# One decoder layer on one core: a planner's figure for GpSimd in the first phase, ranks of the steps around the filling products, and one product moved up in the feed-forward part

## The chip, the core and the metric

The kernel runs on one NeuronCore of a Trainium2 chip as one launch. The metric is the device time of the launch in microseconds (us), from the profiler's first to last instruction and what lies around it; lower is better. TensorE is called PE here, VectorE DVE, ScalarE ACT, GpSimd POOL, and SyncE, which issues most DMAs, SP.

## What is computed

One layer over 2048 positions of width 1024, in float32, batch 1. Cut to what matters:

```python
hn = rms_norm(x, norm1_g)
q, k, v, u = split(hn @ w_in)                    # 512 columns each
attn = diff_attention(rope(q), rope(k), v, lam)  # 4 heads, two causal softmax maps each, difference of the maps
attn = rms_norm(attn, subln_g) * 0.2
y = gelu(s5_scan(u))                             # 32 groups, 64 complex states each
ssm = y * sigmoid(y @ w_glu + b_glu)             # GLU
h = x + concat(attn, ssm) @ w_out                # output projection
hn = rms_norm(h, norm2_g)
h = h + (silu(hn @ w_gate) * (hn @ w_up)) @ w_down   # DFF = 2816
return rms_norm(h, final_g)
```

## The kernel before, in words

A float32 product is made of three single-pass products (`mm3`, lines 518 to 520): each operand is split into a high part, rounded to the fast type by ACT, and a low part, the difference, made by DVE or POOL. So every operand of PE costs an ACT step and a DVE or POOL step first.

**The planner.** Nothing is issued in the order in which it is written. Each step is a `Task` with its engine (or several to choose from), an estimated cost, the tasks that it depends on, the buffers that it takes and gives (`Ring`) and a rank `pri`. `Sched.run` simulates the engines while the program is built: for each engine it looks at the tasks that could start within 0.05 us of the earliest, takes the one of lowest `pri`, and emits it. The result is a fixed order for every engine; on the chip each engine works through its own list in order and waits where an operand isn't there. A task that may run on DVE or POOL goes where its estimated start plus weighted cost is lower (`choose`).

**First phase** (lines 550 to 1000; all its instructions are shown as line 364, which records them; `pri` -100 to -40). RMSNorm, transposes on PE, the projections of u, q, k and v, tables for the scan, and sixteen pairs of scan groups (`ssm_pair`). In a pair, PE makes a product z from operands that are loaded from DRAM (`uD`, `GD`), two multiplies by a table may go to DVE or POOL (`nc.any`), and six 128x256 multiplies and adds for the table are on POOL. `Rec.call` estimates each recorded instruction from its size.

**Second phase.** Attention has `pri` 0 to about 32: scores (lines 1199, 1200, 1203), the row maximum on DVE (1221), exp on ACT (1237), the difference of the two maps on DVE or POOL (1287 to 1291), transposes (1320), the low part on DVE (1329), the product with v, and the heads' norm (1364 to 1382). Its query tiles come by SP from `qD` into a ring of two buffers.

Beside it run the *filling products*, so called because their ranks, 1000 and more, let PE take them only where no attention product can start:
- `glu` (`pri` from 1000): load y, split it, 384 matmuls of 128x256, tanh, multiply (line 1523), store.
- `outproj` (`pri` from 2000): load w_out and split it (high part on ACT, low part on DVE, line 1589), load and split the mixed rows (1609, 1610), 768 matmuls of 128x512 into bank `fx` (after attention into the score banks too); twelve of them make a half tile, which DVE adds to the residual (1645). The first 384 are for the scan's half, the others for attention's half.
- `norm2`: for each of the 16 tiles after its attention half is added: store, square (1676), scale on DVE (1679), transpose on PE (1691), copy (1694), store to `nD`.

**Feed-forward** (`ffn`, `pri` from 10000). Two blocks of 1024 positions; each pair of weight tiles is multiplied by a block with seven products instead of eight (Strassen-Winograd): A11, S2, A12, S3, S1, A22, S4 by B11, T2, B21, T3, T1, B22, T4. A product is 12 matmuls of 128x512 in two tasks of six. Operands of the weights are made in `operands` (s1, s3, s2, s4 on DVE or POOL, lines 1899 to 1909; low parts in 1783 and 1787) and wait in the ring `Ar`; those of the block are made once per block (`inputs_first`, `inputs_second`; lines 1783 and 1796). `blocks` issues the products: A11 into a bank, ACT copies that bank (p1, line 1952), S2 goes to another bank and DVE adds p1 (u2, line 1946), and A12 is accumulated onto A11's bank, for which p1 must have been read. After the two blocks the same scheme runs over w_down in three chunks (`down`), with the final norm in the last.

Of the kernel before, what the change touches and what calls it, by code (L numbers as in the profile page):

```python
# [175 lines left out]
class Sched:  # L176
# [14 lines left out]
    def __call__(self, engs, cost, fn, *deps, take=(), give=(), pri=0.0, size=0, stream=0, of=(), bias=BIAS,  # L191
                 port=False):

        t = Task()
        t.port = port
        t.engs = {engs: cost} if isinstance(engs, str) else engs
        if engs == "pe":
            t.engs = {engs: cost * 1.02}
        else:
            t.engs = {e: c + STEP.get(e, 0.0) for e, c in t.engs.items()}  # L200
        t.fn, t.pri, t.take, t.give, t.size, t.bias = fn, pri, take, give, size, bias
        t.next, t.wait, t.ready, t.done, t.got = [], 0, 0.0, False, {}
        for r in take:
            r.queues.setdefault(stream, deque()).append(t)
        t.at, t.of = stream, [o for o in of if o is not None]
        for d in (*deps, *t.of):
            if d is None:
                continue
            if d.done:
                t.ready = max(t.ready, d.end)  # L210
            else:
                d.next.append(t)
                t.wait += 1
        self.left += 1
        if not t.wait:
            self.arm(t)
        return t
# [79 lines left out]
class Rec:  # L297
# [92 lines left out]
    def call(self, eng, f, args, kw):  # L390
        isap = self.isap
        outs = [kw[n] for n in ("out", "accum_out") if isap(kw.get(n))]
        rest = [x for n, x in kw.items() if n not in ("out", "accum_out") and isap(x)]
        pos = [x for x in args if isap(x)]
        if "out" not in kw:
            outs.append(pos.pop(0))
        ins = rest + pos
        free = lambda x: math.prod(n for _, n in list(x.ap)[1:])
        n = max([free(outs[0])] + ([free(i) for i in ins] if "reduce" in f else []))
        c = ("", f, outs, ins, args, kw)  # L400
        if eng == "pe":
            cost = n / 2400.0 + 0.0035
            if f == "transpose":
                cost = 0.108
            elif kw["rhs"].dtype == F32:
                cost = max(4 * cost, 0.215)
            if self.open and (sum(x[0] for x in self.open) + cost > 1.3
                              or kw.get("start") and self.where(self.open[-1][2][0]) != self.where(outs[0])
                              or self.open[-1][2][0].tensor.name != outs[0].tensor.name):
                self.flush()  # L410
            self.open.append((cost, f, outs, ins, args, kw))
            return None
        self.flush()
        if f == "dma_start":
            return self.task(("sp", 0.47), [c], size=math.prod(outs[0].shape) * 4)
        psum = [x.space == PSUM for x in (outs[0], *ins)]
        if f == "tensor_tensor_scan" or psum[0]:
            dve = 2.3e-3 * n + 0.03
        elif f in ("tensor_scalar", "memset"):
            dve = 0.75e-3 * n + 0.03  # L420
        else:
            dve = 1.06e-3 * n + 0.06 if any(psum) else 1.27e-3 * n + 0.02
        cost = dict(dve=dve, act=0.87e-3 * n + (0.26 if "accum_out" in kw else 0.08),
                    pool=(1.0e-3 if f == "tensor_scalar" else 0.3e-3 if f == "memset" else 2.0e-3) * n + 0.12)
        if kw.get("op") == ALU.pow:
            cost["pool"] += 0.25 + 0.09 * n
        port = f == "tensor_tensor" and not any(psum)
        if eng == "any":
            return self.task({e: cost[e] for e in ("dve", "pool")}, [c], bias=FAIR if self.fair else BIAS, port=port)
        return self.task((eng, cost[eng]), [c], port=port)  # L430
# [69 lines left out]
class K:  # L500
# [1254 lines left out]
    def ffn(self):  # L1755
# [9 lines left out]
        A11, S2, A12, S3, S1, A22, S4 = range(7)  # L1765
# [9 lines left out]
        def pri():  # L1775
            seq[0] += 0.01
            return seq[0]
# [143 lines left out]
        def blocks(ws, B, last, finish):  # L1921
# [22 lines left out]
            def add(x, y, *deps, to=None, give=True):  # L1944

                return S("dve", 1.042e-3 * w + 0.07, lambda t: v.tensor_tensor(  # L1946
                    out=(t if to is None else to).got[tm], in0=x.got[bank], in1=y.got[tm],
                    op=ALU.add), x, y, *deps, take=[tm] if to is None else [], give=[(bank, x)] if give else [], pri=pri())

            place = lambda own: lambda: own.got[tm]  # L1950
            x1 = product(A11)
            p1 = S("act", 0.88e-3 * w + 0.07, lambda t: a_.copy(out=t.got[tm], in_=x1.got[bank]), x1,
                   take=[tm], pri=pri())
            u2 = add(product(S2), p1)
            x2 = product(A12, x1, p1)
            S.join(*finish(0, 0, p1, lambda: x1.got[bank], x2, u2), give=[(bank, x1)])
            u3 = add(product(S3), u2)
            x5 = product(S1)
# [200 lines left out]
        for c, (lo, hi) in enumerate(CHUNKS):  # L2159
            ops = rows(c, 0)  # L2160
            W = columns(c, wide)
            if c == len(CHUNKS) - 1:
                fg.append(S("sp", 0.47, lambda t: nc.sync.dma_start(out=t.got[rawr], in_=A["final_g"]), take=[rawr],
                            pri=pri(), size=524288))
# [29 lines left out]
```

## Time and profile before

| | |
|---|---|
| median of 3 runs | 2428.8 us (2423.4 to 2435.64) |
| the profiled execution | 2427.17 us |
| its span, first to last instruction | 2425.1 us |
| PE busy | 2334.0 us |
| DVE, ACT, POOL busy | 1719.6, 1051.0, 725.1 us |
| mean granted clock of PE | 0.984 |

The profile is of one execution. A row of the waits says who waited for whom, how long in all, how often, and the longest. A row of the windows says, for a stretch, its length, PE's busy time with its matmuls, the granted clock (1.00 is full speed), the DMA engines' share and GB/s. A group's row gives line, engine, operation, out<-in, shapes and count, then busy us and mean ns, then the idle time of the engine before it and what ended it.

### The profile page before, as it was taken

What the parts mean: (1) busy time and instruction counts of PE and PEld (TensorE: products, weight loads), DVE (VectorE), ACT (ScalarE), POOL (GpSimd) and SP (SyncE); (2) the same over time, 40 slices, a digit from 0 to 9 for tenths busy, and PEclk for the clock granted to TensorE, in tenths of its full rate; (3) what the DMA queues carried; (4) which work ended last, traced back from release to release, by engine and by line L of the source; (5) the groups of instructions that cost most, each with busy time, mean ns of one, the idle gap of its engine ahead of it and who ended that gap; (6) DMA issues with size and microseconds to landing.
All of it is one profiled execution on the core that took longest, in us unless ns stands there. A gap on an engine that the chain in (4) does not pass through costs nothing.

```text
span 2425.1 us, 33919 instructions
## 1 busy us (share of the span) xinstructions
PE 2334.0 (96%) x11832; PEld 1958.8 (81%) x11832; DVE 1719.6 (71%) x2801; ACT 1051.0 (43%) x2103; POOL 725.1 (30%) x824
## 2 busy tenths in 40 slices
PE   7999999889999999998999999999999989999998
PEld 6887798878888888876888888788888868878886
DVE  7885775247887768648987666866666677686787
ACT  7222332247877776545332333533333242242343
POOL 4134675355666556545311000100000010010033
PEclk9999999999999999999999999999999999999999
DMA  6467675665566557786986222522322255574564
GB/s 216 133 189 219 220 223 165 202 215 165 191 197 193 194 188 243 228 293 228 304 270 224 86 83 87 204 92 72 95 85 79 87 179 168 172 258 162 201 213 158
DMA packets 312172, 435.33 MB, mean 180 GB/s; under 512 B 42240, under 2 KB 187712, under 8 KB 312000
## 3 DMA queue, kind: packets, MB, share of 16 engines
q1 hardware_dynamic: 309408, 428.71, 55.5%
q10 hardware_dynamic: 2592, 4.45, 0.5%
q8 instruction: 93, 1.52, 0.3%
q14 instruction: 79, 0.65, 0.1%
HBM read 287.66 MB, written 145.42 MB: 179 GB/s over the span
## 4 chain that ended last, share of the span: by engine, by line
PE 70%; DMA 6%; DVE 5%; issue 3%; ACT 2%; POOL 1%; SPq 0%; POOLq 0%; DVEq 0%; ACTq 0%
PE pair L518 9%; PE pair L519 9%; PE pair L520 9%; PE tp L519 4%; PE tp L520 4%; PE tp L518 4%; PE fx L518 4%; PE fx L519 4%; PE pair L364 4%; PE fx L520 4%; PE pv L518 3%; PE pv L519 3%; PE pv L520 3%; DMA hn<-qD 2%; PE tp L1320 2%
## 5 line engine op out<-in xcount | busy, mean ns | idle before, releaser
L1782 ACT CAST misc<-hn 128x512 fp32r<-128x512 f32 (+1 forms) x340 | 204.9, 609 | 482.8 <-PE pair L519 160.6
L519 PE MATMUL pair<-hn,misc 128*128 128x512 f32 x925 | 361.0, 390 | 6.5 <-DVE hn L1783 4.6
L518 PE MATMUL pair<-hn,misc 128*128 128x512 f32 x925 | 361.3, 391 | 3.2 <-DVE misc L1946 2.5
L520 PE MATMUL pair<-hn,misc 128*128 128x512 f32 x925 | 360.2, 389 | 0.0
L1783 DVE TENSOR_TENSOR misc<-hn,misc 128x512 fp32r<-128x512 f32 (+1 forms) x340 | 237.2, 702 | 82.8 <-ACT misc L1782 82.6
L364 PE MATMUL pair<-hn,misc 128*128 128x512 f32 x1152 | 281.7, 398 | 0.0
L1899 POOL TENSOR_TENSOR misc<-hn 128x512 f32<-128x512 f32 (+1 forms) x13 | 17.9, 1378 | 783.0 <-DVE misc L1783 638.2
L364 PEld LDWEIGHTS pair<-hn,misc 128*128 128x128 f32 x1152 | 214.5, 190 | 45.4 <-issue 2.4
L519 PEld LDWEIGHTS pair<-hn,misc 128*128 128x128 f32 x925 | 173.9, 188 | 44.4 <-DVE hn L1783 6.5
L518 PEld LDWEIGHTS pair<-hn,misc 128*128 128x128 f32 x925 | 174.0, 188 | 41.3 <-DVE misc L1946 3.3
L520 PEld LDWEIGHTS pair<-hn,misc 128*128 128x128 f32 x925 | 173.9, 188 | 36.0
L1221 DVE TENSOR_REDUCE small<-pair 128x1 f32<-128x1024 f32 (+7 forms) x160 | 158.2, 991 | 53.5 <-PE pair L1200 24.8
L1237 ACT ACTIVATE hn<-pair,small 128x1024 f32<-128x1024 f32 (+4 forms) x192 | 166.3, 868 | 59.9 <-DVE small L1228 29.1
L519 PE MATMUL tp<-hn,misc 128*128 128x512 f32 x454 | 178.1, 392 | 3.7 <-DVE hn L1783 3.7
L518 PE MATMUL tp<-hn,misc 128*128 128x512 f32 x454 | 177.8, 392 | 0.0
L520 PE MATMUL tp<-hn,misc 128*128 128x512 f32 x454 | 177.4, 391 | 0.0
L1946 DVE TENSOR_TENSOR misc<-pair,misc 128x512 f32<-128x512 f32 x110 | 75.9, 690 | 84.9 <-PE pair L520 84.6
L364 POOL TENSOR_TENSOR misc<-misc,misc 128x512 f32<-128x512 f32 (+1 forms) x71 | 83.9, 1183 | 166.9 <-DVE misc L364 134.1
L364 DVE TENSOR_TENSOR misc<-misc,misc 128x512 f32<-128x512 f32 (+7 forms) x111 | 92.6, 852 | 36.6 <-ACT misc L364 31.9
L1329 DVE TENSOR_TENSOR hn<-tp,hn 128x512 fp32r<-128x512 f32 x144 | 95.4, 684 | 29.0 <-ACT hn L1326 28.6
L364 POOL TENSOR_TENSOR misc<-misc 128x256 f32<-128x256 f32 (+1 forms) x128 | 100.1, 793 | 43.6 <-DVE misc L364 19.8
L364 PE MATMUL pair<-misc,hn 128*128 128x256 f32 x768 | 103.3, 292 | 8.8 <-DVE misc L364 8.8
(272 smaller groups left out, 5614.7 us busy)
## 6 DMA issues: line engine op xcount, KB each, us to landing
hn<-vD SPq DMA_DIRECT2D x48, 512.0 KB
hn<-kD SPq DMA_DIRECT2D x96, 256.0 KB
hn<-in_w_gate SPq DMA_DIRECT2D x44, 512.0 KB
hn<-in_w_up SPq DMA_DIRECT2D x44, 512.0 KB
fD<-misc SPq DMA_DIRECT2D x88, 256.0 KB
misc<-in_w_down SPq DMA_DIRECT2D x77, 256.0 KB
hn<-qD SPq DMA_DIRECT2D x128, 128.0 KB
hD<-misc SPq DMA_DIRECT2D x32, 512.0 KB
```

The source lines that it names most:

```text
L364: getattr(ENGINE[t.at](self.real), f)(*map(now, args), **{n: now(x) for n, x in kw.items()})
L518: nc.tensor.matmul(out, lhsT=ah, rhs=bh, start=start, stop=False, **k)
L519: nc.tensor.matmul(out, lhsT=ah, rhs=bl, start=False, stop=False, **k)
L520: nc.tensor.matmul(out, lhsT=al, rhs=bh, start=False, stop=stop, **k)
L1221: v.tensor_reduce(out=nl[:, i:i + 1], in_=x.got[sc][:, 0:w], axis=AX.X, op=ALU.max, negate=True)
L1237: a_.activation(out=z.got[rings[i]][:, 0:w], in_=x.got[sc][:, 512 * i:512 * i + w], func=AF.Exp, bias=st(n, n + 1), accum_out=acc)
L1320: nc.tensor.transpose(t4[:, kt, t], a[:, kc % 1024:kc % 1024 + 128], self.ident)
L1329: v.tensor_sub(out=y.got[zr][:, 1], in0=y.got[tp].rearrange("p (k q) -> p k q", k=2), in1=y.got[zr][:, 0].bitcast(F32))
L1782: hf = lambda t: a_.copy(out=dst(t)[0], in_=src())
L1783: lf = lambda t: (g_ if t.at == "pool" else v).tensor_sub(out=dst(t)[1], in0=src(), in1=dst(t)[0].bitcast(F32))
L1899: s1 = any_(n, lambda t, e: e.tensor_tensor(out=t.got[s1r][:, 0:n], in0=q(1, 0), in1=q(1, 1), op=ALU.add), *r, take=[s1r], pri=pri(), bias ...
L1946: return S("dve", 1.042e-3 * w + 0.07, lambda t: v.tensor_tensor(out=(t if to is None else to).got[tm], in0=x.got[bank], in1=y.got[tm], op ...
```

## The change

Three edits.
1. In `Sched.__call__`, every task with a rank from 1000 up to 3000 that isn't for PE gets the rank -1. So all DMAs, ACT, DVE and POOL steps of `glu`, `outproj` and `norm2` come ahead of attention's on their engines when both could start; their products on PE keep their ranks. The first phase's ranks (-100 to -40) stay ahead of both.
2. In `Rec.call`, the estimate of a recorded two-input instruction on POOL goes from 2.0 to 2.4 ns an element. Only the first phase is recorded.
3. In `blocks`, product A12 is written ahead of S2, so it has the lower rank. It still needs p1.

```diff
         t.fn, t.pri, t.take, t.give, t.size, t.bias = fn, pri, take, give, size, bias
+        if 1000 <= pri < 3000 and "pe" not in t.engs:
+            t.pri = -1.0
...
-                    pool=(1.0e-3 if f == "tensor_scalar" else 0.3e-3 if f == "memset" else 2.0e-3) * n + 0.12)
+                    pool=(1.0e-3 if f == "tensor_scalar" else 0.3e-3 if f == "memset" else 2.4e-3) * n + 0.12)
...
+            x2 = product(A12, x1, p1)
             u2 = add(product(S2), p1)
-            x2 = product(A12, x1, p1)
```

No instruction is added or removed; the planner gives every engine another order and some steps another engine. Lines after 201 are two higher in the changed kernel. Three places follow.

DVE in attention, where w_out's low parts (line 1589, `misc0`<-`misc2`) are made, between the last GLU step and the first add of a half tile. Before:

```order
L1589 SCALAR_TENSOR_TENSOR misc0_5783<-misc2_5785,misc0_5783 128x512
L1287 SCALAR_TENSOR_TENSOR hn31_4411<-hn31_4411,small_128 128x512
L1221 TENSOR_REDUCE small_128<-pair00_3730 128x1
L1589 SCALAR_TENSOR_TENSOR misc0_5783<-misc2_5785,misc0_5783 128x512
L1287 SCALAR_TENSOR_TENSOR hn31_4411<-hn31_4411,small_128 128x512
L1221 TENSOR_REDUCE small_128<-pair10_4451 128x1
L1329 TENSOR_TENSOR hn10_4054<-tp1_104,hn10_4054 128x512
L1329 TENSOR_TENSOR hn30_4410<-tp0_103,hn30_4410 128x512
L1228 TENSOR_TENSOR small_128<-small_128 128x1
L1589 SCALAR_TENSOR_TENSOR misc0_5783<-misc2_5785,misc0_5783 128x512
```

The changed kernel at the same step (line 1591):

```order
L1223 TENSOR_REDUCE small_128<-pair10_4465 128x1
L1230 TENSOR_TENSOR small_128<-small_128 128x1
L1591 SCALAR_TENSOR_TENSOR misc0_5564<-misc2_5566,misc0_5564 128x512 x4
L1591 SCALAR_TENSOR_TENSOR misc0_5564<-misc5_5569,misc0_5564 128x512 x2
L1591 SCALAR_TENSOR_TENSOR misc3_5567<-misc5_5569,misc3_5567 128x512
L1371 SCALAR_TENSOR_TENSOR small_128<-small_128 128x4
L1223 TENSOR_REDUCE small_128<-pair10_4465 128x1
L1373 SCALAR_TENSOR_TENSOR small_128<-small_128 128x4
L1230 TENSOR_TENSOR small_128<-small_128 128x1
```

The eight low parts stood among 27 rows, between attention's maxima (1221) and low parts (1329); now seven stand in a row, and the eighth a few rows on. From the last GLU multiply to the first add of a half tile it was 47 rows and is 31.

DVE at the start of the feed-forward part, where the block's operands are split (line 1783 into `hn00`, `hn10`: B11 and B21) beside the half tiles' adds (1645) and norm2's scaling (1679). Before:

```order
L1645 TENSOR_TENSOR misc2_5785<-pair10_9454,misc2_5785 128x512
L1783 TENSOR_TENSOR hn00_9652<-hn31_9659,hn00_9652 128x512
L1679 SCALAR_TENSOR_TENSOR misc1_5784<-misc2_5785,misc6_5789 128x1024
L1645 TENSOR_TENSOR misc5_5788<-pair11_9455,misc5_5788 128x512
L1783 TENSOR_TENSOR hn00_9652<-hn31_9659,hn00_9652 128x512
L1645 TENSOR_TENSOR misc5_5788<-pv_105,misc5_5788 128x512
L1783 TENSOR_TENSOR hn10_9654<-hn31_9659,hn10_9654 128x512
L1783 TENSOR_TENSOR hn00_9652<-hn31_9659,hn00_9652 128x512
```

The changed kernel (1647, 1681 and 1785 are the same three):

```order
L1647 TENSOR_TENSOR misc5_5569<-pv_105,misc5_5569 128x512
L1681 SCALAR_TENSOR_TENSOR misc1_5565<-misc2_5566,misc6_5570 128x1024
L1785 TENSOR_TENSOR hn10_9891<-hn31_9896,hn10_9891 128x512
L1647 TENSOR_TENSOR misc5_5569<-pair00_9664,misc5_5569 128x512
L1785 TENSOR_TENSOR hn00_9889<-hn31_9896,hn00_9889 128x512
L1785 TENSOR_TENSOR hn10_9891<-hn31_9896,hn10_9891 128x512
L1785 TENSOR_TENSOR hn00_9889<-hn31_9896,hn00_9889 128x512
L1785 TENSOR_TENSOR hn10_9891<-hn31_9896,hn10_9891 128x512
```

Between the first of these splits and the first add of the feed-forward part (1946) DVE had 53 steps for feed-forward operands, 18 adds and 10 scalings; now it has 48, 5 and 3. The other adds and scalings come earlier.

DVE in the middle of the first block, where the weights' sums are made (1899 is s1, 1901 is s3). Before:

```order
L1946 TENSOR_TENSOR misc6_10374<-pair10_9454,misc1_10373 128x512
L1783 TENSOR_TENSOR misc3_5786<-misc2_5785,misc3_5786 128x512
L1899 TENSOR_TENSOR misc2_5785<-hn31_9659 128x512
L1901 TENSOR_TENSOR hn31_9659<-hn31_9659 128x512
L1787 SCALAR_TENSOR_TENSOR misc3_5786<-hn31_9659,misc3_5786 128x512
L1946 TENSOR_TENSOR misc6_10374<-pair00_9448,misc6_10374 128x512
```

The changed kernel:

```order
L1785 TENSOR_TENSOR misc0_5564<-hn31_9896,misc0_5564 128x512
L1785 TENSOR_TENSOR misc0_5564<-misc2_5566,misc0_5564 128x512
L1948 TENSOR_TENSOR misc6_10351<-fx_106,misc1_10350 128x512
L1789 SCALAR_TENSOR_TENSOR misc0_5564<-hn31_9896,misc0_5564 128x512
L1903 TENSOR_TENSOR hn31_9896<-hn31_9896 128x512
L1948 TENSOR_TENSOR misc6_10351<-tp0_103,misc6_10351 128x512
```

s1 (now 1901) no longer stands ahead of s3 (now 1903): of the 60 sums s1 of 128x512, DVE had 53 and POOL 7; now DVE has 16 and POOL 44. On PE, the first half of S2, all of A12 and the second half of S2 now follow each other in many blocks.

## The prediction, made blind

> **What bounds the kernel now.** I read the page first, then PE's windows by stage, PE's waits, and the timeline at two gaps.
>
> ```profile
> PE 2334.0 (96%) x11832; PEld 1958.8 (81%) x11832; DVE 1719.6 (71%) x2801; ACT 1051.0 (43%) x2103; POOL 725.1 (30%) x824
> ```
>
> PE is busy for 96% of the span, and the change adds and removes no matmul. So only two things can be won or lost: PE's idle time, and matmuls at a lowered clock. The windows place both.
>
> ```profile
> core 0: us, PE busy (x), PEclk, DMA share, GB/s
> 180.00:300.00 120.00, 112.51 (x565) 0.96 0.72 219
> 300.00:430.00 130.00, 128.04 (x781) 0.99 0.64 193
> 430.00:500.00 70.00, 61.12 (x450) 0.95 0.70 213
> 500.00:640.00 140.00, 130.44 (x948) 0.98 0.55 170
> 640.00:668.00 28.00, 22.48 (x139) 0.88 0.82 264
> 668.00:975.00 307.00, 302.10 (x1869) 1.00 0.64 202
> 975.00:1010.00 35.00, 30.10 (x184) 0.90 0.84 251
> 1060.00:1160.00 100.00, 89.87 (x404) 0.95 0.77 256
> 1160.00:1550.00 390.00, 390.00 (x1721) 1.00 0.52 167
> 1550.00:1580.00 30.00, 28.05 (x116) 0.94 0.80 278
> 1580.00:1970.00 390.00, 390.00 (x1722) 1.00 0.29 88
> 1970.00:2010.00 40.00, 32.75 (x120) 0.91 0.65 214
> 2140.00:2180.00 40.00, 35.81 (x135) 0.87 0.69 232
> ```
>
> I call a stage's loss its idle time plus (1 - PEclk) times its length: what it would save if PE never stopped. First phase, 180 to 500: idle 7.5 + 2.0 + 8.9 and clock 4.8 + 1.3 + 3.5, 28 us. Attention's beginning, 500 to 668: idle 9.6 + 5.5, clock 2.8 + 3.4, 21 us. The rest of attention, 668 to 1010: 4.9 + 4.9 and 3.5, 13 us. The passage into the feed-forward part, 1060 to 1160: 10.1 and 5.0, 15 us. The feed-forward blocks have no loss in 780 of their 810 us; the joints at 1550, 1970 and 2140 lose 24 us together. A matmul of 128x512 takes 390 / 1721 = 0.227 us there, a product of twelve 2.72 us.
>
> The clock term needs its own look, at the joint at 1550: the timeline's row at the gap, then a window just behind it.
>
> ```profile
> 1562.64 0.79 PE L519 MATMUL fx<-hn,misc 128*128 128x512 f32 x1 [1.90 <-DVE hn L1783]
> 1562.50:1565.90 3.40, 3.26 (x8) 0.50 0.84 276
> ```
>
> One gap of 1.90 us is followed by 3.4 us at half clock: 1.7 us more are lost. [...] The sum goes by the rows.
>
> PE's waits name the causes: 500 to 640 first (two rows), then 640 to 668 (one), then 180 to 500 (three).
>
> ```profile
> PE pair L1199 <- DMA hn<-qD: 4.7, 5, 1.8
> PE pair L1199 <- ACT hn L1237: 3.3, 2, 2.8
> ...
> PE pair L1199 <- ACT hn L1237: 4.2, 2, 2.3
> ...
> PE pair L364 <- DVE misc L364: 8.8, 5, 3.0
> PE pv L364 <- DMA misc<-uD: 5.6, 8, 1.3
> PE pv L364 <- DMA misc<-GD: 3.5, 1, 3.5
> ```
>
> They are many small waits at places where PE's list stood on an operand that came later than planned. None is a stage's steady limit.
>
> **Part 1, ranks.** No work goes away; steps of the filling products overtake attention's on DVE, ACT, POOL and SP. What stands behind an overtaking step waits for its length, 0.7 us on DVE, and attention behind it; PE covers that as long as a filling product can start. The clearest place is 640 to 668. There GLU was done and the output projection hadn't begun, as DVE's rows of the three kinds show (last GLU multiply, first low part of w_out, first add of a half tile):
>
> ```profile
> L1523 DVE SCALAR_TENSOR_TENSOR misc<-misc x6: 678/702/1111, 516.1 to 637.2; 128x512 f32<-128x512 f32 x6
> L1589 DVE SCALAR_TENSOR_TENSOR misc<-misc,misc x16: 665/684/1770, 651.8 to 960.6; 128x512 fp32r<-128x512 f32 x16
> L1645 DVE TENSOR_TENSOR misc<-fx,misc x42: 667/687/692, 675.6 to 1107.6; 128x512 f32<-128x512 f32 x42
> ```
>
> From 637.2 to 675.6, 38.4 us, there was little to fill with, and 8.9 us were lost. In PE's order 45 of attention's score matmuls stood between the last GLU and the first output projection matmul; now 22 do, and GLU ends after 186 of the 768 instead of 222. I take half of the 8.9: -4.5 us. In 500 to 640 GLU is also further on at every point (120 instead of 72 of its 384 matmuls when 48 score matmuls are done). Its waits are on qD and exp, though, which fills help only where PE's list has them ahead of the late product: a quarter of 12.4, -3. SP is passed too: the filling products' loads and stores now go ahead of the query tiles'. If that doubled the 4.7 us, it would be +5; if fills stood ahead of all of them, -5. For 500 to 668 I take -7.5 us, between -14 and +8. For 668 to 1010, where fills were already there, -2, between -8 and +10 (qD again).
>
> The price comes afterwards. At the end of attention 591 output projection matmuls are done instead of 483. These 108 (24.5 us) used to cover the preparation of the feed-forward operands. Four groups of DVE from 1041 to 1160:
>
> ```profile
> L1679 DVE SCALAR_TENSOR_TENSOR misc<-misc,misc 128x1024 f32<-128x1024 f32 x12 | 20.8, 1737 | 9.8 <-PE tp L1691 5.0 <-POOL misc L570 4.9
> L1783 DVE TENSOR_TENSOR hn<-hn,hn 128x512 fp32r<-128x512 f32 x20 | 16.8, 866 | 2.8 <-ACT hn L1782 2.7
> L1783 DVE TENSOR_TENSOR misc<-hn,misc 128x512 fp32r<-128x512 f32 x13 | 10.0, 803 | 0.7 <-ACT misc L1782 0.7
> L1796 DVE TENSOR_TENSOR hn<-hn,hn 128x512 f32<-128x512 f32 x8 | 6.5, 814 | 0.0
> ```
>
> A step of preparation is (16.8 + 10.0 + 6.5) / 41 = 0.81 us, a scaling 1.74, an add 0.69. DVE's list from the first split to the first feed-forward add was 53 x 0.81 + 18 x 0.69 + 10 x 1.74 = 73 us; it is 48 x 0.81 + 5 x 0.69 + 3 x 1.74 = 48 us. PE's list beside it was 18 half tiles, 49 us, and 60 feed-forward matmuls, 14 us, and some transposes; it is 5 half tiles, 14 us, the same 14 and some 4 of transposes. So DVE was ahead of PE by little and is now longer by 48 - 32 = 16 us, which PE would stand idle, with some clock: 18 against today's 15. I take +3 us. If PE could start none of its feed-forward matmuls before all is split, it is 48 - 14 - 4 = 30 us idle and 6 of clock, 36 against 15: +21. If the operands are split while the earlier half tiles run, nothing: then today's loss goes in part, -8.
>
> **Part 2, POOL's estimate.** POOL's groups of the first phase, then DVE's of the same multiplies:
>
> ```profile
> L364 POOL TENSOR_TENSOR misc<-misc 128x256 f32<-128x256 f32 x121 | 92.6, 776 | 29.4 <-DVE misc L364 19.8 <-DMA misc<-ED 5.1
> L364 POOL TENSOR_TENSOR misc<-misc,misc 128x512 f32<-128x512 f32 x39 | 61.2, 1571 | 67.4 <-DVE misc L364 51.1 <-ACT misc L364 12.0 <-PE tp L364 3.7
> L364 DVE TENSOR_TENSOR misc<-misc,misc 128x512 f32<-128x512 f32 x37 | 33.8, 924 | 15.4 <-ACT misc L364 14.9
> ```
>
> With its 0.13 for a step the planner had 0.76 us for 256 columns and 1.27 for 512, and gets 0.86 and 1.48. The trace has 0.776 and 1.571: the rarer size is now nearer, the commoner is overshot. Six multiplies of 128x512 go from POOL to DVE (POOL 39 to 33 in its order), 6 x 0.924 = 5.5 us of DVE, which has room: the waits of PE here are on DMAs and, from 430, on v's weights (L364 <- DVE, 8.8), which this doesn't touch. Later planned products would find uD landed: up to -5.6 and GD's -3.5 with its clock; a re-ordered list can also wait anew at as many places. I take -2 us, between -14 and +10, half of the loss up or a third of it on top.
>
> **Part 3, A12 ahead of S2.** ACT's copy p1 still stands between A11 and A12, and PE has S2's first half for it; the order shows that half in between. No cost: the blocks run at 1.00 with no idle, and weights' operands wait long before use. The page's row of their high parts on ACT, and DVE's and POOL's s1:
>
> ```profile
> L1782 ACT CAST misc<-hn 128x512 fp32r<-128x512 f32 (+1 forms) x340 | 204.9, 609 | 482.8 <-PE pair L519 160.6
> L1899 DVE TENSOR_TENSOR misc<-hn x55: 543/692/1758, 1113.8 to 2317.5; 128x512 f32<-128x512 f32 x53, 128x384 f32<-128x384 f32 x2
> L1899 POOL TENSOR_TENSOR misc<-hn x13: 1013/1591/1824, 1163.6 to 2392.5; 128x512 f32<-128x512 f32 x7, 128x384 f32<-128x384 f32 x6
> ```
>
> ACT waits for PE to give slots back, not PE for ACT. Thirty-seven s1 that go from DVE to POOL take 1.591 instead of 0.692, 33 us in all, hidden by that stock; if the cover were gone, 33 us. The joints can move either way by a product's half, 1.4 us each: 0, between -6 and +8 with the end.
>
> **Sum.** -7.5 - 2 + 3 - 2 + 0 = -8.5. Against the profiled execution's 2427.2 that is 2418.7; this execution lies 1.6 below the median 2428.8, so 2420 for the median. A difference under 0.5%, 12 us, can hardly be told from none for this kernel.
>
> **Rivals.**
> *The gaps before the feed-forward part mostly close.* For it: fills are further on everywhere, and each gap closed saves its half clock too. Against: many waits sit in front of a product that PE's list puts ahead of the fills. With -8 in the first phase, -14 to 668, -5 to 1010 and 0 after: -27, 2402.
> *The feed-forward part starts uncovered.* Place: the passage after attention. For it: five half tiles of cover instead of eighteen. Against: B11 and B21 are split first, and A11 needs only B11. Price +21 with nothing won elsewhere: 2450. It decides against the change once the passage's idle and clock loss exceed today's 15 by 12 us and what the earlier stages win, so from 27 to 40 us.
> *GpSimd's sums become the limit.* The price is the 33 us above, with the sum's other terms 2453; against it stands ACT's row. [...]
> That the ranks do nothing is excluded by the order.
>
> **Chances.** Forecast, within 0.5%: 0.45. Gaps close: 0.37, counted as faster. Uncovered start: 0.16, and POOL's sums 0.02, both slower. The bounds of the terms on one side, taken as independent, are roots of sums of squares: downwards sqrt(6.5² + 6² + 11² + 12² + 6²) = 19, upwards sqrt(15.5² + 12² + 18² + 12² + 8²) = 30. From 2420 this is 2401 to 2450; the two slower cases hold 0.18, so I cut the upper end to 2444, and the lower, 2401, nearly holds the faster rival's own 2402. The forecast's own range is 2417 to 2441, as wide as its class.
>
> **What would show it.** Right: the loss at the GLU passage halves; the passage into the feed-forward part loses 15 to 20 us; the blocks after it stay at 1.00 with no idle; first phase's waits of another make-up but a like sum. Wrong: an idle PE over 27 us in that passage with DVE over 95% busy and splits (L1785) as releasers; waits on POOL's L1901 in the blocks; or a first phase that changes by over 10 us.

## The result, and the profile after

The changed kernel takes **2452.6 us** (median of 5 runs, 2447.9 to 2454.5), the kernel before 2428.1 beside it (5 runs, 2423.0 to 2435.6): ratio 1.0107, 95% interval [1.0091, 1.0122]. It is slower by 1.1%, outside the predicted range, whose upper end was 2444. Rows of the changed kernel and of some experiments have other line numbers; the text names lines by the kernel before.

The page's row of busy times, of the profiled execution, whose span is 2450.8 us (before 2425.1):

```profile
PE 2338.1 (95%) x11832; PEld 1962.0 (80%) x11832; DVE 1699.1 (69%) x2769; ACT 1048.1 (43%) x2096; POOL 773.8 (32%) x861
```

PE has the same 11832 matmuls and is busy 4.1 us longer; all else of the 25.7 us is idle time (2450.8 - 2338.1 = 112.7 against 91.1). Some of DVE's work has moved to POOL. PE's windows show where the time went. First the one window of before that the prediction hadn't cut out, then the changed kernel:

```profile
390.00:440.00 50.00, 49.96 (x236) 1.00 0.46 147
```

```profile
core 0: us, PE busy (x), PEclk, DMA share, GB/s
180.00:300.00 120.00, 113.67 (x575) 0.96 0.69 203
300.00:390.00 90.00, 86.99 (x587) 1.00 0.75 217
390.00:440.00 50.00, 39.51 (x164) 0.80 0.42 122
440.00:500.00 60.00, 51.96 (x359) 0.94 0.66 199
500.00:640.00 140.00, 127.28 (x917) 0.95 0.56 179
640.00:668.00 28.00, 23.89 (x130) 0.82 0.95 292
668.00:975.00 307.00, 302.04 (x1824) 1.00 0.64 199
975.00:1010.00 35.00, 35.00 (x244) 1.00 0.84 249
1010.00:1060.00 50.00, 45.08 (x294) 0.97 0.78 241
1060.00:1160.00 100.00, 85.01 (x441) 0.91 0.72 239
1190.00:1580.00 390.00, 385.89 (x1701) 1.00 0.49 161
1610.00:1990.00 380.00, 380.00 (x1678) 1.00 0.27 85
```

By the prediction's measure, idle time plus (1 - PEclk) times the length, the first phase from 180 to 500 loses 27.9 + 18.4 = 46 us in place of 28, and 20.5 of them lie in the 50 us from 390 on, where before nothing was lost. From 500 to 668 it is 29 in place of 21, from 668 to 1010 it is 5 in place of 13, from 1010 to 1060 it is 6 in place of 0 (before, PE is busy for all of the 50 us), from 1060 to 1160 it is 24 in place of 15. The measure also counts a lowered clock while PE stands idle (in the change the clock is at 0.50 from 399.5 to 416.6, and PE is busy for 10.68 of these 17.1 us), so these losses add up to more than the time. The blocks of the feed-forward part run at 1.00; the first of them has 4.1 us of idle time, where before there was none.

Since everything after 400 us is shifted, fixed points serve better than fixed windows: the scans of the pairs (line 364 on DVE), the scores (1199) and the second norm's transposes (1691), each with its first and last start at the end of the row's first half. Before, then after:

```profile
L364 DVE TENSOR_TENSOR_SCAN misc<-r,misc x32: 657/677/1103, 240.2 to 397.0; 128x256 f32<-128x256 f32 x32
L1199 PE MATMUL pair<-hn x136: 277/393/767, 470.4 to 1018.9; 128*128 128x512 f32 x90, 128*128 128x256 f32 x34, 128*128 128x384 f32 x12
L1691 PE MATMUL tp<-cst,misc x128: 270/272/472, 992.3 to 1142.3; 128*128 128x128 f32 x128
```

```profile
L366 DVE TENSOR_TENSOR_SCAN misc<-r,misc x32: 658/676/1101, 250.1 to 414.0; 128x256 f32<-128x256 f32 x32
L1201 PE MATMUL pair<-hn x136: 277/392/794, 491.0 to 1074.3; 128*128 128x512 f32 x90, 128*128 128x256 f32 x34, 128*128 128x384 f32 x12
L1693 PE MATMUL tp<-cst,misc x128: 270/273/447, 940.7 to 1169.9; 128*128 128x128 f32 x128
```

The first score starts 20.6 us later (491.0 against 470.4). From there to the last transpose of norm2 it is 678.9 us in place of 671.8, +7.1, and from there to the end 1280.9 in place of 1282.8, -1.9. These points don't cut PE's list at the same place in both kernels. Counted as matmuls of 128x512 at 0.227 us (two of 128x256 are one), the changed kernel's list has 12 more ahead of the first score, 24 fewer in the middle and 12 more in the rest. Without this shift of work it loses 17.9 us ahead of the first score (20.6 - 2.7) and 12.5 in the middle (7.1 + 5.4), and wins 4.6 in the rest (-1.9 - 2.7). So the largest part, 17.9 of the 25.7, is lost before attention begins. PE's timeline just ahead of that shows how. Before, around the last pairs (`pv` is z, `fx` and `tp` are the rest of a pair, `pair<-hn,misc` are projections):

```profile
382.86 5.61 PE L364 MATMUL pair<-hn,misc 128*128 128x512 f32 x24
388.31 0.51 PE L364 MATMUL pv<-misc 128*128 128x256 f32 x3
...
393.09 4.51 PE L364 MATMUL pair<-hn,misc 128*128 128x512 f32 x19
397.53 0.62 PE L364 MATMUL fx<-misc,misc 64*128 64x256 f32 x3
```

After:

```profile
397.80 0.98 PE L366 MATMUL fx<-misc,misc 128*128 128x256 f32 x3
399.01 1.07 PE L366 MATMUL tp<-misc,misc 128*128 128x256 f32 x3 [0.23 <-ACT misc L366]
403.85 0.98 PE L366 MATMUL pv<-misc 128*128 128x256 f32 x3 [3.77 <-DMA misc<-uD]
404.76 1.01 PE L366 MATMUL fx<-misc,misc 64*128 64x256 f32 x3
...
411.09 0.58 PE L366 MATMUL fx<-misc,misc 64*128 64x256 f32 x1 [1.47 <-ACT misc L366]
```

Before, PE does 24 and 19 projection matmuls between the products of the last pairs; after, it has pairs only, and waits again and again, longest (3.77 us) for a load of `uD`. The order of PE says the same. In its list, in which a run of equal matmuls is one row, the changed kernel has at rows 1221 to 1233

```
1221 L366 MATMUL fx_106<-misc4_2024,misc3_2021 128x256 x6
1222 L366 MATMUL pv_105<-misc3_2021 128x256 x6
1223 L366 MATMUL tp1_104<-misc4_2024,misc3_2021 128x256 x6
1224 L366 MATMUL fx_106<-misc3_2021,misc4_2024 128x256 x3
1225 L366 MATMUL tp1_104<-misc3_2021,misc4_2024 128x256 x3
1226 L366 MATMUL pv_105<-misc3_2021 128x256 x3
1227 L366 MATMUL fx_106<-misc4_2024,misc3_2021 128x256 x6
```

and so on, with no projection between the last pairs. The first pair's z stands at row 729 (before 699), the last one's at 1231 (before 1208), and behind the first score 168 projection matmuls are left (before 192: one tile of 24 has moved ahead).

### The profile page after: what moved, and what is told of

Its sections match the earlier page's. It is cut to its first block, busy times and chain, and to the rows that moved or that the text cites. A ratio compares the mean times of both kernels' runs of the same rounds, so it can differ in the third digit from the quotient of the medians.

```text
span 2450.8 us, 33935 instructions
## 1 busy us (share of the span) xinstructions
PE 2338.1 (95%) x11832; PEld 1962.0 (80%) x11832; DVE 1699.1 (69%) x2769; ACT 1048.1 (43%) x2096; POOL 773.8 (32%) x861
## 4 chain that ended last, share of the span: by engine, by line
PE 67%; DMA 6%; DVE 4%; issue 2%; ACT 1%; POOL 1%; SPq 1%; POOLq 0%; DVEq 0%; ACTq 0%
PE pair L521 8%; PE pair L520 8%; PE pair L522 8%; PE tp L521 4%; PE tp L522 4%; PE tp L520 4%; PE fx L520 4%; PE fx L522 4%; PE fx L521 4%; PE pv L520 3%; PE pv L521 3%; PE pv L522 3%; DMA hn<-qD 3%; PE tp L1322 2%; PE pair L1201 2%; PE pair L1202 2%
## 5 line engine op out<-in xcount | busy, mean ns | idle before, releaser
L1901 POOL TENSOR_TENSOR misc<-hn 128x512 f32<-128x512 f32 (+1 forms) x50 | 68.6, 1372 | 814.3 <-DVE misc L1785 633.1
L366 POOL TENSOR_TENSOR misc<-misc,misc 128x512 f32<-128x512 f32 (+1 forms) x65 | 76.9, 1184 | 185.9 <-DVE misc L366 143.1
L1331 DVE TENSOR_TENSOR hn<-tp,hn 128x512 fp32r<-128x512 f32 x144 | 96.1, 684 | 28.4 <-ACT hn L1328 27.9
L520 PE MATMUL fx<-misc,misc 128*128 128x512 f32 (+1 forms) x280 | 105.9, 378 | 5.5 <-DVE misc L1647 3.9
```

The source lines that it names most:

```text
L366: getattr(ENGINE[t.at](self.real), f)(*map(now, args), **{n: now(x) for n, x in kw.items()})
L520: nc.tensor.matmul(out, lhsT=ah, rhs=bh, start=start, stop=False, **k)
L1331: v.tensor_sub(out=y.got[zr][:, 1], in0=y.got[tp].rearrange("p (k q) -> p k q", k=2), in1=y.got[zr][:, 0].bitcast(F32))
L1901: s1 = any_(n, lambda t, e: e.tensor_tensor(out=t.got[s1r][:, 0:n], in0=q(1, 0), in1=q(1, 1), op=ALU.add), *r, take=[s1r], pri=pri(), bias ...
```

## The experiments

The first question was which part lost the time. Theory A: the first phase, through part 2. Theory B: the passage into the feed-forward part, through part 1's ranks (the prediction's rival "starts uncovered"). Four runs, beside the kernel before at 2424.1 us.

**Part 2 alone.**
```diff
-                    pool=(1.0e-3 if f == "tensor_scalar" else 0.3e-3 if f == "memset" else 2.0e-3) * n + 0.12)
+                    pool=(1.0e-3 if f == "tensor_scalar" else 0.3e-3 if f == "memset" else 2.4e-3) * n + 0.12)
```


> The kernel before with part 2 alone (2.4 ns an element for GpSimd's two-input steps of the first phase). Theory A, the first phase lost the time: the pairs of scan groups start about 9 us later and their last store comes 15 to 20 us later, first-phase matmuls end near 530 instead of 508, and the whole is 2440 to 2448 us. Theory B, the passage into the feed-forward part lost it: 2424 to 2433 us, first phase ends within 6 us of before.

Measured: 2459.6 us, ratio 1.0150 [1.0129, 1.0170]; more than the whole change, and above theory A's own range.

**Part 1 alone.**
```diff
+        if 1000 <= pri < 3000 and "pe" not in t.engs:
+            t.pri = -1.0
```


> The kernel before with part 1 alone (the ranks). Theory A: the first phase is as before, the GLU passage loses less and the passage into the feed-forward part more; 2424 to 2436 us. Theory B: the passage into the feed-forward part loses 27 us or more instead of 15, 2440 to 2450 us.

Measured: 2434.4 us, 1.0053 [1.0035, 1.0070].

**Part 3 alone.**
```diff
+            x2 = product(A12, x1, p1)
             u2 = add(product(S2), p1)
-            x2 = product(A12, x1, p1)
```


> The kernel before with part 3 alone (A12 ahead of S2). Both theories: no idle in the middle of the blocks, joints within 3 us, 2424 to 2432 us. A third theory, that the joints lose by it: over 2434 us, with idle at 1550 to 1580 and 1970 to 2010 above 15 us together instead of 9.

Measured: 2420.7 us, 0.9988 [0.9978, 0.9998]; below all of the expected ranges, by little.

**Parts 1 and 3** (the two diffs above together).

> The changed kernel without part 2 (parts 1 and 3 stay). Theory A: the first phase is that of before and the whole is 2424 to 2438 us. Theory B: 2445 to 2453 us, as the changed kernel.

Measured: 2430.7 us, 1.0018 [1.0007, 1.0028]. So theory A: part 2 loses by itself 35 us, and the change without it only some 4 to 7. B falls as the main cause.

**How does an estimate lose time?** In part 2's list for POOL two things strike. Four of the first pair's table steps stand ahead of the last steps that prepare the tables (theory S, a late start), and in the pairs six table steps stand in a row between two 128x512 multiplies, of which fewer are left to POOL (theory T). Two runs split the estimate by size, one holds the table steps back, and one delays POOL in the kernel before without telling the planner. The kernel before took 2424.9 beside them.

**The estimate for 128x512 alone.**
```diff
-... else 2.0e-3) * n + 0.12)
+... else 2.4e-3 if n >= 512 else 2.0e-3) * n + 0.12)
```


> Kernel before with GpSimd's new estimate (2.4 ns) for its 128x512 multiplies alone; its 128x256 steps keep 2.0. In the order the table steps then stand as in the kernel before around the last preparation steps, but later, in the pairs, they stand six in a row between two 128x512 multiplies, as with the whole estimate. Theory S (late start: the table steps ahead of the last preparation steps delay the first pair by some 10 us, and the chain of sixteen pairs hands that on): first scan near 240 us as before, time 2424 to 2436. Theory T (six table steps in a row hold up the multiply of every pair, the chain gets longer): last scan 405 or later, time 2444 to 2462. Half and half: 2436 to 2446 here and in the next run.

Measured: 2451.5 us, 1.0106 [1.0083, 1.0129]; scans 240.8 to 410.0.

**The estimate for the smaller size alone.**
```diff
+... else 2.0e-3 if n >= 512 else 2.4e-3) * n + 0.12)
```


> The other half: 2.4 ns for GpSimd's 128x256 steps alone. Four table steps then stand ahead of the last preparation steps, as with the whole estimate, and in the pairs mostly three between two multiplies, as before. Theory S: first scan near 250 us, time 2444 to 2462. Theory T: time 2424 to 2436, last scan at most 5 us later than before. The prediction's reading (GpSimd's waits in the first phase are covered one by one by other work): both runs 2424 to 2430.

Measured: 2461.1 us, 1.0147 [1.0121, 1.0172]; scans 248.9 to 415.9.

**Part 2 alone, the first pair's table steps held back.**
```diff
+                if hf == 1 and q0 == NG - 2:
+                    v.tensor_copy(out=self.mark, in_=H_[:, 0, 0, 0:1])
...
+        if n == 0:
+            v.tensor_copy(out=ed[:, 0, 0:1], in_=self.mark)
         nc.sync.dma_start(out=ed, in_=self.ED[hf][:, n8])
```


> GpSimd's whole estimate, but the first pair's table steps are made to wait for the last preparation step (one small copy on VectorE, read by another, some 0.1 us each). Theory S: first scan near 242 us, and most of the loss of the estimate alone (2459.6) goes: 2426 to 2442. Theory T: the loss stays, 2448 to 2462, though the first scan is early again.

Measured: 2465.0 us, 1.0164 [1.0141, 1.0188]; scans 242.4 to 413.4. The early start is back and brings nothing: S falls. (Of the two halves, the first had come out as T said and the second as S said, so neither theory explained both.)

**POOL delayed, the order untouched** (`rep` makes the emitting function issue a call so many times; the planner sees one).
```diff
+                nc.rep = 13 if hf == 1 and q0 == NG - 2 else 1
                 g_.tensor_tensor(out=U, in0=f1(im, 8), in1=f2(c2), op=ALU.mult)
+                nc.rep = 1
```


> Kernel before, its order untouched: one of the last preparation multiplies of GpSimd (128x256, 0.78 us) is issued 13 times in a row in place of once, unknown to the planner, so that GpSimd comes to the last preparation steps 12 x 0.78 = 9.3 us later. The computed values are the same. Chain theory: all sixteen pairs shift by 6 to 10 us, the fill on TensorE runs out ahead of the last of them, and the time is 2434 to 2450. The prediction's reading (GpSimd's work in the first phase is covered): 2424 to 2430.

Measured: 2427.2 us, 1.0007 [0.9995, 1.0020]; scans 242.4 to 399.0. Nine microseconds more of POOL shift the first scan by 2.2 and the time by nothing. So this delay of POOL is covered, in keeping with the prediction's reading of PE's waits. What isn't covered is a planner that believes in a slower POOL. Both halves of the estimate had lost, with different POOL lists, which speaks against T too. What all the losing runs share is PE's list: the last pair's z at rows 1231 to 1234, and 168 matmuls left behind the first score.

**Theory P**, then: PE issues in the order of its list (in the change's timeline above, the products at 397.80, 399.01 and 403.85 come as rows 1224 to 1226 have them, and the last of them starts only after 3.77 us of idle time). A longer *planned* chain of pairs makes the planner fill PE with more projections ahead of each pair's products. The real chain is held to that order, the projections are used up before the last pairs, and those, and attention's beginning, find no cover. It would not matter where the longer plan comes from, and a longer *real* chain would cost little. Four runs, the kernel before at 2425.7 beside them.

**The scan's estimate raised, POOL's left alone.**
```diff
-        if f == "tensor_tensor_scan" or psum[0]:
-            dve = 2.3e-3 * n + 0.03
+        if f == "tensor_tensor_scan":
+            dve = 3.4e-3 * n + 0.03
+        elif psum[0]:
+            dve = 2.3e-3 * n + 0.03
```


> Kernel before with GpSimd's estimate left at 2.0, but the planner's estimate of VectorE's scan raised from 2.3 to 3.4 ns per element (two scans of 256 to each pair, so 16 x 2 x 0.28 = 9 us more of planned chain). No work changes, nor where GpSimd's steps stand ahead of the first pair. Theory P (TensorE's queue: a longer planned chain puts more projection matmuls ahead of each pair's products; TensorE issues in order, so the real chain is held to the plan, and the projections are used up before the last pairs): the last pair's product stands at place 1231 of TensorE's list in place of 1208, as with GpSimd's whole estimate, so TensorE starves between 390 and 440 us and the time is 2438 to 2456. Theory T (what costs is that GpSimd does fewer of the 128x512 multiplies and its table steps stand in sixes): 2422 to 2432, since neither is changed by more than a step or two.

Measured: 2451.4 us, 1.0109 [1.0089, 1.0129]; 168 matmuls left. T falls: POOL's estimate isn't touched, and the loss is there. It lies elsewhere, though. PE's window of 390 to 440 in this run:

```profile
390.00:440.00 50.00, 45.60 (x204) 1.00 0.47 137
```

Here 4.4 us are lost, at full clock, where the change loses 20.5; PE's list still has 24 and 29 projection matmuls between some of the last products. The first score comes 10.7 us later than before, and more, 13.7 us, is lost behind it, up to the last transpose of norm2. So the starved last pairs are where the change loses most, but not what every longer plan brings; why attention loses as much isn't shown.

**POOL's estimate at 1.6** (2.0e-3 becomes 1.6e-3).

> GpSimd's estimate lowered to 1.6 ns in place of raised, further from the trace. The last pair's product stands at place 1191 of TensorE's list (before 1208). Theory P: the chain of pairs ends by 3 to 8 us earlier, nothing starves: 2412 to 2430. Theory of an estimate that should be near the trace (a wrong one costs both ways): 2432 to 2445.

Measured: 2429.0 us, 1.0014 [1.0003, 1.0024]; 192 left. No gain, but an estimate that lies further from the trace costs nearly nothing on this side.

**POOL's estimate at 2.2.**

> GpSimd's estimate at 2.2 ns, half of the step. The first pair's product stands at place 707 of TensorE's list (before 699, after 729), the last at 1233 (before 1208, after 1231). Theory P: the last place decides, so nearly the whole loss is there: 2444 to 2462. If the loss grows with the estimate or with the late start: 2434 to 2442.

Measured: 2449.0 us, 1.0098 [1.0081, 1.0115]; 168 left. Half of the step has two thirds of the loss: it comes in a jump.

**A longer real chain.**
```diff
+        nc.rep = 2
         v.tensor_tensor(out=t1, in0=pq, in1=Cb, op=ALU.mult)
+        nc.rep = 1
```


> Kernel before, its order untouched: the first multiply of each pair on VectorE (128x512, 0.92 us) is issued twice, unknown to the planner; the computed values are the same. 16 x 0.92 = 15 us more of real chain. If the real chain of the pairs sets the first phase's end: the last scan comes 10 to 15 us later (407 to 412), TensorE starves ahead of it, 2440 to 2456. If VectorE has room there (it is busy about two thirds of that stage) and TensorE's queue sets the pace: last scan at most 5 us later, 2424 to 2434.

Measured: 2428.5 us, 1.0016 [1.0006, 1.0025]. The row of the scans, here with line numbers two higher:

```profile
L366 DVE TENSOR_TENSOR_SCAN misc<-r,misc x32: 656/676/683, 239.2 to 401.4; 128x256 f32<-128x256 f32 x32
```

Fifteen microseconds more of DVE in the chain end it 4.4 later, and 2.8 come through to the time. So this longer real chain is nearly covered.

All this goes with PE's order, but the order had not been set by itself. For that, PE's 536 tasks of the first phase were numbered as they are made, their order taken down in one kernel, and forced upon the other: a task of that list may only start when it is the next.

**Part 2's estimate with PE's order of before**, and **the estimate of before with PE's order of part 2**.
```diff
+FIRST = [a + d * k for a, n, d in (
+    (24, 6, 3), (188, 1, 0), (42, 2, 3), (189, 4, 1), (71, 6, 3), (212, 1, 0), (89, 2, 3), (213, 2, 1),
...
+        if t.id in self.held and t.id != self.first[0]:
+            return None
```


> GpSimd's whole estimate (as the run of part 2 alone, 2459.6), but the first phase's 536 tasks of TensorE are held to the order that they have in the kernel before: first pair's product again at place 699, last at 1208, 192 projection matmuls left behind the first score. GpSimd, VectorE and ScalarE stay as the new estimate sorts them: table steps in sixes, eight fewer of the 128x512 multiplies on GpSimd. Theory P (TensorE's order is what costs): 2422 to 2436. Theory T (GpSimd's own order and share cost): 2445 to 2462.

> The converse: kernel before with its estimate of 2.0, but the first phase's 536 tasks of TensorE are held to the order that the new estimate gives (first pair's product at place 729, last at 1231, 168 matmuls left behind the first score). GpSimd keeps its multiplies (no fewer than before). Theory P: 2445 to 2464. Theory T: 2424 to 2438.

Measured, beside 2426.1 for the kernel before: 2427.1 us, 1.0002 [0.9990, 1.0014], and 2452.5 us, 1.0117 [1.0100, 1.0135]. PE's window of 390 to 440, of the first and of the second:

```profile
390.00:440.00 50.00, 49.34 (x231) 1.00 0.45 146
```

```profile
390.00:440.00 50.00, 39.67 (x163) 0.80 0.41 117
```

The first is the row of the kernel before (49.96, x236, 1.00), the second that of the change (39.51, x164, 0.80). With the estimate fixed, PE's order takes the loss away or brings it. One thing these two runs don't separate: a planner that is held to a list for PE fits the other engines' lists to it. In the first phase, part 2 alone takes 66 of SP's 320 steps and 57 of ACT's 314 out of the order that they have in the kernel before; with PE held to the order of before it is 19 and 14. So what is shown is PE's order with the lists that go with it, SP's order of loads among them, and not PE's list by itself.

**The ranks by halves.** What part 1 costs was to be split: its first half with part 3, its second half alone.
```diff
+        if 1000 <= pri < 2000 and "pe" not in t.engs:
+            t.pri = -1.0
```


> Part 3 with half of part 1: only the gated unit's steps (due times 1000 to 2000) get the rank -1, not the output projection and the second norm (2000 to 3000). If the new ranks lose in the passage into the feed-forward part alone, through the output projection's steps: 1060 to 1220 us loses as before (15 us of idle time and clock), 640 to 700 us some 2 to 4 us less, and the time is 2414 to 2424, below part 3 alone or beside it. If the gated unit's rank is what costs: 2428 to 2438.

Measured: 2444.9 us, 1.0078 [1.0057, 1.0100]. Missed: the gated unit's ranks alone cost more than all the ranks together, between the first score and the last transpose of norm2 (692.3 us in place of 671.8).
```diff
+        if 2000 <= pri < 3000 and "pe" not in t.engs:
+            t.pri = -1.0
```


> The other half of part 1 alone: rank -1 for the output projection's and the second norm's steps (2000 to 3000) only. If these cost: the waits of the second norm's transposes for ScalarE and VectorE in 1060 to 1220 us stand at 8 to 12 us as with the whole of part 1, and the time is 2430 to 2440. If not: 2424 to 2430.

Measured: 2429.4 us, 1.0022 [1.0012, 1.0032]: at the edge between the two, and the loss of 1060 to 1220 is 21 us, between 15 before and 25 with all the ranks. The halves don't add up.

**The whole change with PE's order of before in the first phase.** The list of the run above, put into the changed kernel.

> The whole change, with the first phase's 536 tasks of TensorE held to the order of the kernel before. If the order of the first phase's matmuls is all that part 2 costs in the change, this comes to what parts 1 and 3 give without it (2430.7): 2426 to 2436, 16 to 26 us below the change (2452.6). If GpSimd's new estimate costs in the change by another way too: 2438 to 2452.

Measured: 2449.3 us, 1.0098 [1.0085, 1.0111], beside 2425.7. The first expectation is missed, and with it the claim that this order is all that part 2 costs in the change. The first score is at 471.3 again and the last transpose of norm2 at 1145.4, both as in parts 1 and 3 alone (471.5 and 1147.0). But from there to the end it takes 1303.3 us, where no other run took more than 1287. Half of that is work: PE's list has 5532 matmuls of 128x512 behind that transpose, the kernel before 5484, and the 48 more are 10.9 us. So of the 1303.3 - 1282.8 = 20.5 us some 10 are lost there. The middle has as much less work, the worth of 45 matmuls or 10.2 us, so that its 674.1 us in place of 671.8 hide a loss of 12.5. PE's waits from 1130 to 1221 in this run:

```profile
PE pair L575 <- DVE misc L2003: 5.2, 2, 3.3
PE pair L576 <- DVE hn L1840: 3.8, 2, 3.5
PE tp L1748 <- DVE misc L1736: 3.7, 1, 3.7
PE pair L575 <- ACT hn L1839: 3.7, 2, 2.3
```

And PE's window of 75 us from that transpose on, in this run and then in the change:

```profile
1146.00:1221.00 75.00, 65.97 (x262) 0.91 0.82 276
```

```profile
1170.00:1245.00 75.00, 70.89 (x310) 0.99 0.86 282
```

L2003 is here the feed-forward add (1946 before), L1736 norm2's scaling (1679), and L1839 and L1840 the high and low parts of the feed-forward operands (1782 and 1783). So the feed-forward part starts in part uncovered, the prediction's second rival, but at about half of its price; the other half of what this run loses lies between the first score and that transpose. Why the planner comes to that list with the new ranks and the new estimate, and not with the ranks alone, has not been tried and stays open.

**Part 3 alone, again.**

> Part 3 alone once more, with more rounds, as the fastest version so far (2420.7 beside 2424.1): 2418 to 2424, ratio 0.997 to 1.000. If the first time was chance: 0.999 to 1.002.

Measured: 2425.0 us beside 2425.7, 0.9994 [0.9983, 1.0005]. It is the fastest version seen, but not faster by anything that can be told.

The runs side by side. "First score" is the first start of line 1199, "middle" from there to the last start of 1691, "rest" from there to the end of the span. These are of the profiled execution, whose time can differ from the median by some us:

| | us | last scan | first score | middle | rest |
|---|---|---|---|---|---|
| before | 2428.1 | 397.0 | 470.4 | 671.8 | 1282.8 |
| the change | 2452.6 | 414.0 | 491.0 | 678.9 | 1280.9 |
| part 2 alone | 2459.6 | 417.5 | 497.0 | 684.0 | 1283.3 |
| scan's estimate raised | 2451.4 | 405.6 | 481.1 | 685.5 | 1282.9 |
| POOL at 2.2 | 2449.0 | 406.0 | 484.9 | 682.1 | 1282.6 |
| PE's order of part 2, estimate of before | 2452.5 | 409.7 | 487.6 | 684.6 | 1279.2 |
| part 2, PE's order of before | 2427.1 | 397.9 | 469.6 | 673.3 | 1279.8 |
| longer real chain | 2428.5 | 401.4 | 471.9 | 673.2 | 1279.0 |
| parts 1 and 3 | 2430.7 | 397.1 | 471.5 | 675.5 | 1286.0 |
| the change, PE's order of before | 2449.3 | 396.6 | 471.3 | 674.1 | 1303.3 |

## Why the prediction was wrong

**The step that failed** is the term "Part 2, POOL's estimate: -2 us, between -14 and +10". It measured +20.6 at the first score, +18 without the tile of projections that moved ahead of it, and +18 by the windows of 180 to 500. Over the whole kernel part 2 costs some 22 us in the change (2452.6 against 2430.7 without it) and 35 alone. The working looked at the engines whose estimate or share changed: the new figure's distance from the trace, six multiplies more on DVE, operands landing sooner or later. None of that was the loss: with the lists of the kernel before, a delayed POOL (2427.2) and more DVE work in the chain (2428.5) are covered or nearly so. But an estimate acts through the planner on every engine's order, PE's as well. For attention the prediction had counted PE's order (45 score matmuls between two fills, then 22); for the first phase it didn't. Rows 699 and 1208 of before against 729 and 1231 were there to be read. Behind this lies a sentence of its first part, that the waits of the first phase are "many small waits" and none "a stage's steady limit". True of the kernel before, it hid that the window from 390 to 440 was full only because projections were left to fill it. With this term set right the forecast would not yet have held: the change with PE's order of before in the first phase is at 2449.3, outside the range as well, and why is open.

**The beginning of attention, -7.5 us.** By the windows 500 to 668 went from 21 to 29. The passage from the last GLU multiply (639.4) to the first add of a half tile (667.4) did get shorter, 28 us in place of 38.4, as read from the order, but 640 to 668 lost 9.1 us (23.89 busy at 0.82) after 8.9 before, so -4.5 became 0. The wait for qD on scores, in the prediction the danger from passing SP's queue, went from 9.6 to 16.0 us over all of attention.

**The rest of attention, -2 us.** 668 to 1010 went from 13 to 5, but attention lasts longer in the change: its last score starts at 1074.3, before at 1018.9. From 1010 to 1060, where nothing was lost, it loses 6, and from 1010 on scores wait 9.0 us for qD. So there is no gain of 8: most of it is given back by 1060, and the danger that the prediction had named for this term, qD, did come.

**The passage into the feed-forward part, +3 us, between -8 and +21.** By the same window, 1060 to 1160, +9 (24 against 15). The passage lies 27 us later in the change, though (last transpose at 1169.9, before at 1142.3), so that this window ends before it does; from 1060 to 1220, which takes in both, it is 33 against 15, +18, with attention's last waits in it. The sign was right and the middle too low; the bound held. The releasers are not the splits that had been named but norm2's scaling and copy:

```profile
PE tp L1693 <- DVE misc L1681: 6.8, 1, 6.8
PE tp L1693 <- ACT misc L1696: 4.3, 2, 4.0
```

With PE's order of before in the first phase the splits are among the releasers, as the rival had it, but with the moved work taken off, some 10 us are lost behind the last transpose, half of the rival's +21.

**Part 3 and POOL's sums, 0.** Right in the main. Part 3 alone is at 0.9988 and 0.9994, and the 44 sums on POOL, at 1.292 in the median, hold up nothing that shows: no wait of PE from 1190 on names them. The first block has two others, 2.7 us for p1 (the row below) and 1.4 for a feed-forward add:

```profile
PE pv L520 <- ACT misc L1954: 2.7, 1, 2.7
L1901 POOL TENSOR_TENSOR misc<-hn x50: 1012/1292/5844, 1182.0 to 2418.3; 128x512 f32<-128x512 f32 x44, 128x384 f32<-128x384 f32 x6
```

The text named a first phase that changes by over 10 us as a sign that it would be wrong. That is what came, but no rival stood for it, and the range ended 9 us short.

## What to carry to other kernels

Where a planner fixes the order, an estimate is a priority. Ask first what it does to the order of the engine that is the bound, and count there how much fill stands ahead of the last step of each chain that runs beside it; fill spent early is missing at the chain's end and at the start of the next stage. A figure nearer to the trace is no better for that. With the planner's fixed 0.25 us, 2.0 ns gave 0.76 us for 256 columns and 1.27 for 512, against 0.776 and 1.571 in the trace; raised to 2.4 for the 512 columns alone, 1.48, it is nearer to the trace, and the time went to 2451.5. All steps at 1.6, 2.0, 2.2 and 2.4 ns gave 2429, 2426, 2449 and 2460 us. So here an optimistic figure for work on a chain cost next to nothing, and a pessimistic one held the chain to the plan. And undoing the cause of a loss in one stage need not give the time back: with PE's order of before in the first phase the change had its 20 us ahead of attention again, and lost as much behind it, some 12 us by the last transpose of norm2 and some 10 after it.

## What the runs showed of the hardware

In the change the clock fell ahead of the longest gap of that stretch. It stands at half from 399.5 to 416.6, 17.1 us, and in the 3.5 us ahead of that PE was busy for 2.94, with no gap over 0.59 us; the gap of 3.77 came later:

```profile
396.00:399.50 3.50, 2.94 (x14) 1.00 0.17 25
399.50:416.60 17.10, 10.68 (x43) 0.50 0.49 135
416.60:417.20 0.60, 0.60 (x4) 1.00 0.62 65
```

So the records show PE busy for 84% (2.94 / 3.50) of the 3.5 us before the fall. The run with the estimate of before and PE's order of part 2 has a fall at about the same place:

```profile
390.00:395.00 5.00, 4.22 (x24) 1.00 0.27 77
395.00:400.00 5.00, 1.04 (x4) 0.53 0.77 186
400.00:405.00 5.00, 5.00 (x24) 0.50 0.67 184
```

There PE was busy for 84% (4.22 / 5.00) of the 5 us up to 395, and the 0.53 of the next 5 us puts the fall at some 395.3, an estimate that takes the clock as 1.00 before and 0.50 after. What makes the clock fall, and what sets the length of the 17.1 us, these runs don't show.
